# Bias rows loaded one unit ahead, and the weights of eleven attention units formed by VectorE into DRAM

## The chip, the cores and the metric

The kernel runs on one core of a Trainium2 chip. Its engines are TensorE (PE; its weight loads are shown as PEld), VectorE (DVE), ScalarE (ACT), GpSimd (POOL) and the DMA engines; nearly all DMAs are issued by SyncE (SP), whose queue is worked off in order, so a DMA that waits for something holds back all that stand behind it. The metric is the device time of one execution in microseconds (us). The kernel before takes 2162.34 us (median of three runs, 2156.7 to 2164.05).

## The reference

A decoder trunk of two layers on one sequence of 1024 positions with 1024 features, all float32. Layer 0 mixes positions by a gated MLP, layer 1 by dilated attention; each is followed by an MLP with squared ReLU (width 4096), with RMSNorm ahead of each part and at the end. The change concerns the attention:

```python
WINDOW_DILATIONS = ((128, 1), (512, 4), (2048, 16))
ATT_HEADS, HEAD_DIM = 8, 64
qkv = (h @ w_qkv).reshape(B, S, 3, N_DIL_GROUPS, ATT_HEADS, HEAD_DIM)
...
# for each of the three groups (window, dilation), with blk = window // dilation:
s = jnp.einsum('bnqrhc,bnkrhc->bnrhqk', qb, kc) * (HEAD_DIM ** -0.5)
rel = blk + jnp.arange(blk)[:, None] - jnp.arange(2 * blk)[None, :]
bias = jnp.transpose(bias_table[_t5_bucket(jnp.clip(rel, 0, blk) * dilation)], (2, 0, 1))
logits = jnp.where(valid, s + bias, NEG_INF)
m = jnp.max(logits, axis=-1)
p = jnp.exp(logits - m[..., None])
den = jnp.sum(p, axis=-1)
num = jnp.einsum('bnrhqk,bnkrhc->bnqrhc', p, vc)
# the groups' outputs are merged per head with weights exp(m - m_all), then
o = (num_sum / den_sum[..., None]).reshape(B, S, ATT_WIDTH)
return o @ w_out
```

The bias of a logit depends only on the distance of query and key, so for each head and group it is one row of numbers, and a tile of biases is that row shifted by one for each partition.

## The kernel before

*Arithmetic.* A float32 matmul is made of three fp32r matmuls: each operand is split into a rounded part `hi` and a rest `lo`, and hi*hi, hi*lo and lo*hi are added up in one PSUM bank. `split` (L211, L212) does this: ACT rounds (`hi`), and DVE, or the engine that is handed in, subtracts (`lo`). Large products use a scheme with seven half-size products of sums of blocks instead of eight; so "formed" weights are the four quarter blocks of a matrix, added and subtracted (four operations) into seven operands, each split into hi and lo.

*Attention.* It is worked in 12 units, four pairs of heads by three groups, the groups in the order 1, 2, 0 (`ORDER`). Unit i in the function `unit_qk(i)` makes its queries and keys by seven products with the weights w[1], 6, 5, 2, 7, 3, 4; `total` adds banks, `halves` splits the results into `q` and `k`. While these products run for unit i, generators work on the unit before: `scorer` (L1260 adds the bias and takes the maximum on DVE, L1262 takes the exponential on ACT), `turner` (transposes P and splits it), `valuer` (P times V, out of the bank by L1300 on ACT and L1301 on DVE into `N`), `exchange` (softmax statistics through DRAM: `sc`, back as `ex`, L1377) and `merge`. Before the units, `all_values` makes V for all units and writes it to DRAM (`vd`), from which `v_load` brings the part of one unit (L1155 to L1161).

*Weights of the units.* Units listed in `PREPARED` are formed early by `prepare`, with DVE's adds, split and written to DRAM (`wd`, L481); in the attention `unit_weights` only loads them (L1081). The first list is formed in the last part of the first mixer, the second in `all_values`. Units 0, 3, 6 and 9 are in neither: for these `unit_weights` loads the four raw blocks and forms them with GpSimd just before use (L1091 to L1100, and the `lo` of `split`). A unit's weight is brought by `more()`, seven ahead of use, into one of eight buffers.

*Bias.* `bias_tile` loads, at the start of each unit, the bias row of two heads from DRAM (`bvec`), each partition shifted by one (L1027; for group 2, half of it after a memset, L1030 and L1032), into a buffer `t`. A DVE copy (L1037) reverses it into a buffer `b`, of which there are two.

*What sets the order.* PE's order is written out by a planner (`flow`), which estimates a time for each matmul and lets the generators go on when their due time, in ns in `LAT` and `PACE`, has come. The order on DVE, ACT, POOL and SP comes from a scheduler that goes by the program's order and by priorities (`tc.high_priority`) of the operations that PE waits for. Each engine then works strictly in its order. Temporary half tiles come from a ring of 13 buffers `t` (`temp`, `rtemp`), larger ones from 37 buffers `s` (`slot`), raw weights from four buffers `r` (`raw`): whoever wants a buffer waits for the last use of what was in it, a DMA's landing included.

*The end of the attention.* When the weights have all been brought, `more()` steps through `end_loads`, which brings the outputs of earlier heads (`o<-od`, L1465), the last unit's V, the residual `h` (L1478) and the weights of the output projection (`wlbo`, L518).

## Time and profile before

| | |
|---|---|
| three runs | 2162.34, 2164.05, 2156.7 us |
| the profiled execution | 2172.37 us, its span 2170.6 us |
| busy: PE / DVE / ACT / POOL | 2124.0 / 1612.5 / 1115.9 / 571.3 us |
| granted TensorE clock, mean | 0.99 |
| moved by DMA | 345.65 MB |
| formed weights: written, loaded | 56 and 56 DMAs of 512 KB |
| the bias copies (L1037) | 12, from 1053.5 to 1426.3 us, 294 to 1552 ns each |

All times from a trace are of the profiled execution, which took longer than each of the three runs; differences are worked out within it and then set against the median. The attention's units run from about 1050 to 1510 us of the span. Busy time of PE near its whole share means that nothing can be gained in that stretch but by fewer matmuls; where it is less, or where the granted clock is under 1.00, the rows around that moment tell what PE waited for. "A <- B" in a row of waits reads: A was idle until B came.

### The profile page before, as it was taken

What the parts mean: (1) busy time and instruction counts of PE and PEld (TensorE: products, weight loads), DVE (VectorE), ACT (ScalarE), POOL (GpSimd) and SP (SyncE); (2) the same over time, 40 slices, a digit from 0 to 9 for tenths busy, and PEclk for the clock granted to TensorE, in tenths of its full rate; (3) what the DMA queues carried; (4) which work ended last, traced back from release to release, by engine and by line L of the source; (5) the groups of instructions that cost most, each with busy time, mean ns of one, the idle gap of its engine ahead of it and who ended that gap; (6) DMA issues with size and microseconds to landing.
All of it is one profiled execution on the core that took longest, in us unless ns stands there. A gap on an engine that the chain in (4) does not pass through costs nothing.

```text
span 2170.6 us, 30481 instructions
## 1 busy us (share of the span) xinstructions
PE 2124.0 (98%) x10192; PEld 1750.7 (81%) x10192; DVE 1612.5 (74%) x2965; ACT 1115.9 (51%) x2258; POOL 571.3 (26%) x414
## 2 busy tenths in 40 slices
PE   8999999999999999999999999999999999999997
PEld 7888887888878888788887777777788888788886
DVE  7867668777788776887457676758886667987776
ACT  7644436555564443345366555644455556544442
POOL 2000224333323233510220202001443332432244
PEclk9999999999999999999999999999999999999999
DMA  6324704566555443449734444491254443554432
GB/s 214 127 78 175 262 22 163 194 208 210 197 192 181 148 148 118 157 171 364 276 108 155 108 136 101 150 267 40 88 180 160 155 146 131 190 169 143 147 113 78
DMA packets 197825, 345.65 MB, mean 159 GB/s; under 512 B 36905, under 2 KB 64676, under 8 KB 197668
## 3 DMA queue, kind: packets, MB, share of 16 engines
q1 hardware_dynamic: 188528, 342.34, 47.3%
q10 hardware_dynamic: 9140, 1.36, 0.4%
q8 instruction: 80, 1.31, 0.2%
q14 instruction: 77, 0.63, 0.1%
HBM read 228.12 MB, written 115.51 MB: 158 GB/s over the span
## 4 chain that ended last, share of the span: by engine, by line
PE 79%; DVE 10%; DMA 5%; ACT 4%; issue 2%; POOL 0%; SPq 0%; ACTq 0%; DVEq 0%; POOLq 0%
PE at L183 43%; PE mm L183 35%; DMA t<-bvec 2%; ACT t L1262 1%; DVE tr L212 1%; PE at L190 1%; DVE h L311 1%; DVE N L1301 1%; DVE y L212 1%; DMA sc<-st 1%; DVE h L920 1%; DMA r<-in_w_v 1%; DVE wp L212 1%; DMA r<-in_w_dn 1%; DVE q L1189 1%
## 5 line engine op out<-in xcount | busy, mean ns | idle before, releaser
L211 ACT ACTIVATE wp<-r 128x512 fp32r<-128x512 f32 (+2 forms) x432 | 257.2, 598 | 356.0 <-PE at L183 236.2
L183 PE MATMUL at<-hx,wp 128*128 128x512 f32 x1740 | 406.3, 389 | 2.3 <-DVE h L920 2.0
L183 PEld LDWEIGHTS at<-hx,wp 128*128 128x128 f32 x1740 | 326.4, 188 | 71.6 <-DVE h L920 2.9
L212 DVE TENSOR_TENSOR wp<-r,wp 128x512 fp32r<-128x512 f32 (+2 forms) x404 | 308.3, 768 | 70.4 <-ACT wp L211 66.9
L183 PE MATMUL mm<-y,wp 128*128 128x512 f32 x1344 | 340.8, 396 | 2.0 <-issue 1.2
L183 PE MATMUL at<-t,wp 128*128 128x512 f32 x1344 | 313.7, 389 | 0.0
L183 PEld LDWEIGHTS mm<-y,wp 128*128 128x128 f32 x1344 | 249.8, 189 | 55.6 <-issue 2.2
L183 PEld LDWEIGHTS at<-t,wp 128*128 128x128 f32 x1344 | 252.3, 188 | 52.3
L354 POOL TENSOR_TENSOR t<-r 128x512 f32<-128x512 f32 (+3 forms) x62 | 87.7, 1414 | 580.6 <-DMA r<-in_w_dn 262.6
L267 POOL TENSOR_TENSOR t<-t 128x512 f32<-128x512 f32 (+1 forms) x64 | 84.3, 1317 | 440.2 <-ACT t L262 437.9
L183 PE MATMUL mm<-hx,wp 128*128 128x512 f32 x696 | 169.6, 390 | 0.4 <-DVE b L939 0.4
L183 PE MATMUL mm<-t,wp 128*128 128x512 f32 x576 | 158.7, 413 | 0.0
L183 PE MATMUL mm<-y,whi 128*128 128x512 f32 x512 | 158.2, 390 | 0.0
L212 DVE TENSOR_TENSOR hx<-t,hx 128x512 fp32r<-128x512 f32 x192 | 146.8, 771 | 11.6 <-ACT hx L211 11.3
L183 PEld LDWEIGHTS mm<-hx,wp 128*128 128x128 f32 x696 | 130.2, 188 | 29.3 <-issue 1.1
L211 ACT ACTIVATE hx<-t 128x512 fp32r<-128x512 f32 x192 | 118.8, 627 | 46.2 <-DMA t<-hid 40.0
L920 DVE TENSOR_TENSOR h<-h,at 128x512 f32<-128x512 f32 x144 | 98.0, 681 | 55.2 <-PE at L183 54.7
L183 PEld LDWEIGHTS mm<-t,wp 128*128 128x128 f32 x576 | 105.6, 194 | 22.2 <-issue 0.2
L183 PE MATMUL at<-y,wp 128*128 128x512 f32 x480 | 118.7, 390 | 0.0
L183 PEld LDWEIGHTS mm<-y,whi 128*128 128x128 f32 x512 | 95.6, 188 | 19.6
L1262 ACT ACTIVATE t<-t,st 128x128 f32<-128x128 f32 (+1 forms) x192 | 84.3, 440 | 44.7 <-DVE st L1260 44.0
L356 POOL TENSOR_TENSOR r<-r 128x512 f32<-128x512 f32 (+3 forms) x62 | 91.9, 1482 | 54.8 <-DVE wp L212 46.6
(210 smaller groups left out, 3561.5 us busy)
## 6 DMA issues: line engine op xcount, KB each, us to landing
t<-hid SPq DMA_DIRECT2D x182, 256.0 KB, 4.4
hid<-t SPq DMA_DIRECT2D x140, 256.0 KB, 2.3
r<-in_w_up SPq DMA_DIRECT2D x120, 256.0 KB, 2.7
wd<-wq SPq DMA_DIRECT2D x56, 512.0 KB, 3.9
wp<-wd SPq DMA_DIRECT2D x56, 512.0 KB, 3.3
r<-in_w_dn SPq DMA_DIRECT2D x80, 256.0 KB, 2.6
hid<-b SPq DMA_DIRECT2D x56, 256.0 KB, 2.7
r<-in_w_v SPq DMA_DIRECT2D x48, 256.0 KB, 2.9
```

Source lines behind the costliest of these rows:

```text
L183: nc.tensor.matmul(out, lhsT, rhs, **kw)
L190: nc.tensor.transpose(out, src, ident)
L211: nc.scalar.activation(hi, src, AF.Copy)
L212: (engine or nc.vector).tensor_tensor(lo, src, hi.bitcast(F32), op=ALU.subtract)
L267: nc.gpsimd.tensor_tensor(self.acc, self.acc, sq, op=ALU.add)
L311: nc.vector.tensor_tensor(x, x, ps, op=ALU.add)
L354: tt(r3, r[0, 0], r[1, 0], op=ALU.subtract)
L356: tt(r[1, 1], r[1, 0], r[0, 0], op=ALU.subtract)
L920: return engine.tensor_tensor(hs[i, s], hs[i, s], src, op=ALU.add).ins
L1189: nc.vector.scalar_tensor_tensor(lo, src, sc, hi.bitcast(F32), op0=ALU.mult, op1=ALU.subtract)
L1262: nc.scalar.activation(p[:, c], p[:, c], AF.Exp, bias=m, scale=-1.0, accum_out=dn)
L1301: nc.vector.tensor_tensor(o, o, pv[r, c], op=ALU.add)
```

## The change

1. `PREPARED` now lists eleven units in three lists: 1 to 5, then 6, 7, 8 and 10, then 9 and 11. So only unit 0 is formed with GpSimd. The first list starts earlier (ahead of column block 4 of the U product instead of 5 to 7), the third is new: it starts 20 us of the planner's time after the attention begins, at a pace of 3.5 us per step, with raw weights in the four `r` buffers.
2. In `prepare` a formed operand is split into two half tiles of the ring `t` and written as two DMAs of 256 KB, instead of one tile of the ring `s` and one DMA of 512 KB.
3. `bias_tile` only loads; the new `bias_turn` makes the reversed copy. Unit i+1's rows are loaded at the start of unit i, and copied in the middle of unit i, after the last scores of unit i-1.
4. `ex` is loaded 12 instead of 8 us (planned) after the statistics were written.
5. `end_loads` starts with the last unit's V instead of the outputs.

```diff
-PREPARED = ((1, 2, 4, 5), (7, 8, 10, 11))
-PACE = (2100.0, 2500.0, 1900.0)
-LAT = dict(..., ex=8000.0)
+PREPARED = ((1, 2, 3, 4, 5), (6, 7, 8, 10), (9, 11))
+PACE = (2100.0, 2500.0, 1900.0, 3500.0)
+LAT = dict(..., ex=12000.0)
...
-    def prepare(unit_list, pace):
+    def prepare(unit_list, pace, own=temp):
...
-            r00, r10, r01, r11 = (load(w_qkv[n + a][:, half(b)], temp()) for a, b in ((0, 0), (1, 0), (0, 1), (1, 1)))
+            r00, r10, r01, r11 = (load(w_qkv[n + a][:, half(b)], own()) for a, b in ((0, 0), (1, 0), (0, 1), (1, 1)))
             yield pace
             def put(p, src):
-                t = slot((P, 2, HALF), F32R, "wq")
-                split(t[:, 0, :], t[:, 1, :], src)
-                nc.sync.dma_start(wd[i, p], t.bitcast(F32))
+                hi, lo = rtemp(), rtemp()
+                split(hi, lo, src)
+                for e, t in enumerate((hi, lo)):
+                    nc.sync.dma_start(wd[i, p][:, e, :], t.bitcast(F32))
...
-        if tiles[-1] == 7:
+        if tiles[0] == 4:
             flow.add(prepare(PREPARED[0], PACE[0]))
...
+        return rev, w
+
+    def bias_turn(rev, w):
         t = spare().rearrange("p (a b) -> p a b", a=2)
         src = rev[:, 0:2 * w]
         nc.vector.tensor_copy(t[:, :, 0:w], bass.AP(tensor=src.tensor, offset=src.offset + w - 1,
...
-        u.bias = bias_tile(u.hp, g)
+        if i == 0:
+            u.bias = bias_turn(*bias_tile(u.hp, g))
         if i < NU - 1:
             flow.add(v_load(i))
+            U[i + 1].rev = bias_tile(U[i + 1].hp, U[i + 1].g)
...
             flow.until(lambda: U[i - 1].scored.t is not None)
+        if i < NU - 1:
+            U[i + 1].bias = bias_turn(*U[i + 1].rev)
         halves(1, 1, own(total(k1, e, k1), g))
...
     def end_loads():
+        flow.add(v_load(NU - 1))
+        flow.pump()
         for hp in range(2):
             outs_load(hp, 0)
-        flow.add(v_load(NU - 1))
         yield
...
         flow.add(gen())
+    flow.add(prepare(PREPARED[2], PACE[3], raw), 20000.0)
     for i in range(NU):
         unit_qk(i)
```

PE's order is the same in both kernels. The other engines' order moves in three places that matter.

SP's queue around the loads of bias rows for unit 6 before (`V` of units 4 and 5, raw weights `r` of unit 6, statistics `ex`, formed weights `wp` of unit 7, and `t<-bvec` for units 5 and 6):

```order
504 L1377 DMA ex_11646<-sc_11509 128x8x4
505 L1027 DMA t<-bvec 128x2x256
506 L1161 DMA V<-vd_8790 64x4x256 x4
507 L172 DMA r<-in_w_qkv 128x512 x3
508 L1155 DMA V<-vd_8790 128x4x256
509 L172 DMA r<-in_w_qkv 128x512
510 L1377 DMA ex_12009<-sc_11879 128x8x4
511 L1155 DMA V<-vd_8790 128x4x256
512 L1081 DMA wp<-wd_1_140 128x1024
513 L1027 DMA t<-bvec 128x2x256
514 L1081 DMA wp<-wd_6_143 128x1024
```

and now (the first `t<-bvec` holds unit 6's rows, the second unit 7's; `wp` are formed weights of units 6 and 7):

```order
543 L1165 DMA V<-vd_8921 64x4x256
544 L1028 DMA t<-bvec 128x2x256
545 L1085 DMA wp<-wd_1_147 128x1024
546 L1165 DMA V<-vd_8921 64x4x256
547 L1085 DMA wp<-wd_6_150 128x1024
548 L1165 DMA V<-vd_8921 64x4x256 x2
549 L1385 DMA ex_11948<-sc_11789 128x8x4
...
557 L1385 DMA ex_12300<-sc_12141 128x8x4
558 L1085 DMA wp<-wd_1_154 128x1024
559 L1033 DMA t<-bvec 64x2x64 x2
```

The rows of unit 6 are now issued where those of unit 5 were, ahead of `ex`; the raw weights of unit 6 are gone, and loads of formed weights stand among those of `V`.

DVE's order at the copy of unit 6's bias (L1189 is the `lo` of q and k, L1301 the addition into N, L1260 the score reduction, written as ISA):

```order
1352 L1194 TENSOR_TENSOR t<-t,mm 128x512
1353 L1189 SCALAR_TENSOR_TENSOR k_11818<-t,k_11817 128x512
1354 L1037 COPY b<-t 128x512
1355 L1301 TENSOR_TENSOR N<-N,at 64x256 x2
1356 L1260 ISA t,st_11930<-at,b 128x128
1357 L1260 ISA st_11930 128x1
```

and now:

```order
1391 L1309 TENSOR_TENSOR N<-N,at 64x256
1392 L1195 SCALAR_TENSOR_TENSOR k_12081<-t,k_12080 128x512
1393 L1041 COPY b<-t 128x512
1394 L1200 TENSOR_TENSOR t<-t,mm 128x512
1395 L1195 SCALAR_TENSOR_TENSOR q_12007<-t,q_12006 128x512
1396 L1309 TENSOR_TENSOR N<-N,at 64x256 x2
1397 L212 TENSOR_TENSOR tr<-at,tr 128x256 x2
1398 L1200 TENSOR_TENSOR t<-t,mm 128x512
```

The copy has moved up a few rows, and the rows that it copies were asked for a unit earlier.

DVE's order while the scores of unit 0 are reduced and unit 1's products run, before:

```order
1069 L1194 TENSOR_TENSOR t<-t,mm 128x512
1070 L1260 ISA t,st_10068<-at,b 128x128
1071 L1260 ISA st_10068 128x1
...
1076 L1260 ISA t,st_10068<-at,b 128x256
1077 L1260 ISA st_10068 128x1
1078 L1194 TENSOR_TENSOR t<-t,mm 128x512
1079 L212 TENSOR_TENSOR tr<-at,tr 128x384 x2
```

and now (`tr<-r,tr` is the `lo` of a formed weight of unit 9, `r<-r` an addition of its blocks):

```order
1092 L1200 TENSOR_TENSOR t<-t,mm 128x512
1093 L212 TENSOR_TENSOR tr<-r,tr 128x512
1094 L1268 ISA t,st_10265<-at,b 128x128
1095 L1268 ISA st_10265 128x1
...
1100 L1268 ISA t,st_10265<-at,b 128x256
1101 L1268 ISA st_10265 128x1
1102 L486 TENSOR_TENSOR r<-r 128x512
1103 L212 TENSOR_TENSOR tr<-r,tr 128x512
1104 L1200 TENSOR_TENSOR t<-t,mm 128x512
1105 L212 TENSOR_TENSOR tr<-at,tr 128x384 x2
```

Three operations of the new third list stand between the score reductions and the totals; 22 such operations are spread over the first units of the attention.

More of the change, by code (lines that the diff above doesn't have):

```diff
@@ L109 @@
 CALM = (1600.0, 1600.0, 1200.0, 1600.0)
-PREPARED = ((1, 2, 4, 5), (7, 8, 10, 11))
-PACE = (2100.0, 2500.0, 1900.0)
-LAT = dict(sum=2600.0, rms=2600.0, tile=1600.0, gate=8500.0, soft=5500.0, turn=4200.0, fe=1300.0, v=2000.0, qk=4200.0, merge=2600.0, out=700.0, fex=3.0, ve=1600.0, vd=6000.0, ex=8000.0)
+PREPARED = ((1, 2, 3, 4, 5), (6, 7, 8, 10), (9, 11))
+PACE = (2100.0, 2500.0, 1900.0, 3500.0)
+LAT = dict(sum=2600.0, rms=2600.0, tile=1600.0, gate=8500.0, soft=5500.0, turn=4200.0, fe=1300.0, v=2000.0, qk=4200.0, merge=2600.0, out=700.0, fex=3.0, ve=1600.0, vd=6000.0, ex=12000.0)
 @with_exitstack
@@ L465, in start_terms @@
         flow.add((terms.second if s else terms.first)(sq, gi), LAT["sum"])
-    wd = {(i, p): dram.tile([P, 2, HALF], F32, name=f"wd{i}_{p}", bufs=1) for i in PREPARED[0] + PREPARED[1] for p in SEVEN}
-    def prepare(unit_list, pace):
+    wd = {(i, p): dram.tile([P, 2, HALF], F32, name=f"wd{i}_{p}", bufs=1) for i in sum(PREPARED, ()) for p in SEVEN}
+    def prepare(unit_list, pace, own=temp):
         tt = nc.vector.tensor_tensor
```

## The prediction, made before the result was known

> **What bounds the kernel now.** I read the page's busy line and its chain first, then the busy time by stretches of the attention, then the waits, and last the rows in time around each stall of PE.

> ```profile
> PE 2124.0 (98%) x10192; PEld 1750.7 (81%) x10192; DVE 1612.5 (74%) x2965; ACT 1115.9 (51%) x2258; POOL 571.3 (26%) x414
> PE 79%; DVE 10%; DMA 5%; ACT 4%; issue 2%; POOL 0%; SPq 0%; ACTq 0%; DVEq 0%; POOLq 0%
> PE at L183 43%; PE mm L183 35%; DMA t<-bvec 2%; ACT t L1262 1%; DVE tr L212 1%; PE at L190 1%; DVE h L311 1%; DVE N L1301 1%; DVE y L212 1%; DMA sc<-st 1%; DVE h L920 1%; DMA r<-in_w_v 1%; DVE wp L212 1%; DMA r<-in_w_dn 1%; DVE q L1189 1%
> ```

> TensorE is busy for 98% of the span, and POOL, from which the change takes work, has no share in the chain. So only two things can move the time: matmuls, which the change does not touch, and the few places where PE stands or runs slowly. The chain names one of these: 2% for the landing of the bias rows (t<-bvec). The next rows are the attention in stretches of about 54 us: length, then busy time of PE, PEld, DVE, ACT and POOL, the granted clock, the DMA share and GB/s.

> ```profile
> 1086.00:1140.00 54.00, 53.83 (x337) 44.26 (x337) 32.80 (x107) 34.60 (x105) 13.04 (x10) 1.00 0.36 107
> 1140.00:1194.00 54.00, 52.58 (x336) 43.10 (x336) 40.61 (x133) 33.13 (x95) 1.28 (x1) 1.00 0.46 156
> 1194.00:1248.00 54.00, 50.77 (x300) 41.77 (x299) 33.33 (x86) 30.30 (x84) 15.51 (x11) 0.94 0.45 106
> 1248.00:1302.00 54.00, 48.82 (x297) 39.95 (x296) 37.95 (x129) 31.84 (x92) 0.00 (x0) 0.94 0.40 134
> 1302.00:1357.00 55.00, 51.78 (x304) 42.60 (x303) 33.95 (x87) 30.31 (x84) 14.21 (x10) 0.94 0.42 104
> ```

> In the first two stretches PE is nearly full at clock 1.00 and does 336 matmuls. In the next three it does about 300 and the clock is 0.94: there is the loss. The waits of 1085 to 1530 us (total, times, longest) name the cause:

> ```profile
> DVE b L1037 <- DMA t<-bvec: 31.3, 11, 8.3
> PE at L183 <- DVE N L1301: 11.9, 6, 4.6
> PE at L183 <- DMA V<-vd: 2.4, 1, 2.4
> ```

> DVE waits for bias rows, and behind its copy stands the addition N that empties the bank PE wants next. In time, first PE (start, length, and in brackets the idle time before and what ended it), then DVE:

> ```profile
> 1216.56 2.10 PE L183 MATMUL at<-k,q 64*128 64x128 f32 x12 [2.39 <-DVE N L1301]
> 1254.61 2.23 PE L183 MATMUL at<-k,q 64*128 64x256 f32 x12 [4.56 <-DVE N L1301]
> 1325.46 2.10 PE L183 MATMUL at<-k,q 64*128 64x128 f32 x12 [2.38 <-DVE N L1301]
> 1360.14 0.35 PE L183 MATMUL at<-k,q 64*128 64x256 f32 x1 [0.99 <-DVE N L1301]
> 1427.31 0.29 PE L183 MATMUL at<-k,q 64*128 64x128 f32 x1 [1.28 <-DVE N L1301]
> 1441.29 1.84 PE L183 MATMUL at<-tr,V 128*128 128x128 f32 x8 [2.41 <-DMA V<-vd]
> ```

> ```profile
> 1214.01 1.21 DVE L1037 COPY b<-t 128x512 f32<-128x512 f32 x1 [2.23 <-DMA t<-bvec]
> 1252.85 0.43 DVE L1037 COPY b<-t 128x512 f32<-128x512 f32 x1 [8.30 <-DMA t<-bvec]
> 1322.73 1.39 DVE L1037 COPY b<-t 128x512 f32<-128x512 f32 x1 [2.05 <-DMA t<-bvec]
> 1358.38 0.43 DVE L1037 COPY b<-t 128x512 f32<-128x512 f32 x1 [4.74 <-DMA t<-bvec]
> 1426.29 0.43 DVE L1037 COPY b<-t 128x512 f32<-128x512 f32 x1 [3.22 <-DMA t<-bvec]
> ```

> Each of the first five PE gaps ends a microsecond or two after such a late copy. Four of the six gaps are followed by a spell in which the clock is halved; the one in the last row of these is V's, and the fifth row here, after the 0.99 us gap, shows full clock.

> ```profile
> 1216.00:1223.00 7.00, 6.33 (x27) 5.47 (x28) 3.72 (x20) 5.05 (x20) 2.56 (x2) 0.51 0.11 24
> 1253.00:1261.00 8.00, 6.36 (x25) 5.05 (x26) 6.14 (x28) 4.86 (x19) 0.00 (x0) 0.57 0.18 68
> 1325.00:1332.20 7.20, 6.63 (x27) 5.77 (x28) 3.62 (x20) 5.11 (x21) 2.56 (x2) 0.53 0.07 15
> 1441.40:1451.60 10.20, 10.20 (x38) 8.32 (x39) 3.72 (x14) 3.69 (x13) 0.00 (x0) 0.50 1.03 394
> 1360.20:1367.00 6.80, 6.57 (x43) 5.50 (x44) 5.57 (x30) 5.09 (x20) 0.00 (x0) 1.00 0.31 110
> ```

> What a spell costs is its length times what is missing from the clock: 7.00 x 0.49 = 3.4, 8.00 x 0.43 = 3.4, 7.20 x 0.47 = 3.4, and 10.20 x 0.50 = 5.1 us. Gaps of 2.38 us and more bring one, gaps of 1.28 us and less do not.

> **The change, part by part.** *Bias rows a unit ahead.* The DMA keeps its place in the program, but what it loads is now the next unit's rows, and the copy stands in the middle of the unit before its use. Why the rows came late is seen on SP's queue before the worst stall:

> ```profile
> 1243.26 0.38 SPq L1377 DMA_DIRECT2D ex<-sc  x1
> 1243.73 1.74 SPq L1155 DMA_DIRECT2D V<-vd  x1
> 1245.56 0.46 SPq L1081 DMA_DIRECT2D wp<-wd  x1
> 1246.11 0.38 SPq L1027 DMA_DIRECT2D t<-bvec  x1
> ```

> Issued at 1246.11, they were copied at 1252.85, 6.7 us later. A unit lasts about 35 us (copies at 1322.73 and 1358.38), and the copy in the middle of the unit leaves more than 10 us between issue and copy, so even the 8.30 us wait is covered. Without its wait and its own length, the copy lets N run 3.4, 8.7, 3.4, 5.2 and 3.7 us earlier, each more than the PE gap behind it. So all five gaps go: 2.39 + 4.56 + 2.38 + 0.99 + 1.28 = 11.6 us, and their three spells, 10.3 us: -21.9 us. Bounds: -11.6 (the gaps go and the spells stay) and -21.9.

> [...]

> *Units 3, 6 and 9 no longer formed on GpSimd; eleven units formed by DVE.* This takes 33 POOL operations away and adds 33 to DVE; ACT's 7 roundings per unit only move in time.

> ```profile
> L212 POOL TENSOR_TENSOR wp<-r,wp 128x512 fp32r<-128x512 f32 x21 | 28.4, 1351 | 229.0 <-ACT wp L211 229.0
> L212 DVE TENSOR_TENSOR wp<-r,wp 128x512 fp32r<-128x512 f32 (+2 forms) x404 | 308.3, 768 | 70.4 <-ACT wp L211 66.9
> ```

> POOL's 28.4 us in the attention cost PE nothing that the chain shows, so their removal brings 0. Beside POOL's work the bias copy took 1.21 and 1.39 us instead of 0.43, but that is inside the gaps counted already.

> DVE's new operations take 33 x 0.768 = 25 us. Eleven of them go to the first list, which begins earlier in the first layer's mixer and has five units instead of four: 8.4 us. There DVE has room, as in the stretch

> ```profile
> 262.00:278.00 16.00, 16.00 (x72) 13.24 (x71) 1.74 (x4) 1.90 (x3) 3.87 (x3) 1.00 0.21 76
> ```

> with 1.74 us of DVE work in 16 and PE full: cost 0 (if the cover failed, 8.4). The other 22 go to the new third list (units 9 and 11), interleaved with the first units of the attention: 16.9 us. With the 73.4 us that DVE works in 1086 to 1194 this makes 90.3 of 108, and ACT gets 14 roundings more. It has room on average, but the order on DVE is fixed, so that each new operation stands ahead of a score reduction, a total or an N. It also shares the ring of 13 "t" buffers with them, and a buffer is now free only when the write of a weight half to DRAM has landed. The row nearest to such crowding is where DVE was fullest:

> ```profile
> 1165.00:1175.00 10.00, 10.00 (x65) 8.82 (x64) 9.62 (x30) 5.91 (x16) 0.00 (x0) 1.00 0.30 105
> 1175.00:1185.00 10.00, 9.09 (x61) 7.08 (x60) 6.49 (x25) 7.39 (x23) 0.00 (x0) 1.00 0.45 137
> ```

> DVE at 9.62 of 10 cost PE nothing in that stretch and 0.91 us in the next. The third list has two units of eight steps at a pace of 3.5 us, 56 us at the least; I take 80, four such pairs: 3.6 us; and one gap in two chances long enough for a spell, half of 3.4 us: 1.7. I take +5 us. Bounds: 0 (all in DVE's free time) and 16.9 (all on PE's path), before spells.

> *Writes in 256 KB halves instead of 512 KB, and three units more loaded from DRAM.* 56 writes become 154, loads of formed weights go from 56 to 77.

> ```profile
> wd<-wq SPq DMA_DIRECT2D x56, 512.0 KB, 3.9
> SPq L1081 <- PE mm L183: 122.5, 35, 11.1
> ```

> DMA engines are below half busy in all five attention rows above, a write is waited for by a buffer only, and SP mostly waits for PE, since eight weight buffers run ahead: cost 0, bounds 0 to 98 more issues x 0.38 us (a single issue above) = 37 us, if SP's queue were the last to arrive everywhere; the chain gives SP's own queue 0%. [...]

> *The later load of softmax statistics (8 to 12 us) and the order at the end.* ex<-sc no longer holds SP ahead of V and weights: 0, since the bias gap it fed is already counted. The V stall at 1441.29 stays: its V stands behind the same four h loads and two weight loads as before. The bias and ex issues ahead of these go,

> ```profile
> 1418.08 0.78 SPq L1027 DMA_DIRECT2D t<-bvec  x1
> 1423.88 0.58 SPq L1377 DMA_DIRECT2D ex<-sc  x1
> ```

> which is 1.4 us, but PE arrives 1.28 us earlier without the gap at 1427.31. So 0; the bounds are -7.5 (2.41 + 5.1) and 0.

> **Sum.** -21.9 + 5 = -16.9 us. The profiled execution took 2172.4 us and would take 2155.5; it lies 10.0 us above the median of the runs, 2162.3, from which the same difference gives 2145.4: forecast 2145 us. [...] The likeliest case's own range is 2140 (crowding 0) to 2152 (crowding 12).

> **The rivals.** *The spells stay (A).* If the half clock has another cause than the gaps, for instance the short matmuls of 64 rows that follow each of them, only the gaps go: -11.6 + 3.6 = -8, 2154 us. For it speaks that the gaps are shorter than the spells; against it that none of the short matmuls after 0.99 us was slowed.

> *The V stall goes too (B).* Then 2145 - 7.5 = 2138 us. For it: 1.4 us less stands ahead on SP; against it: PE comes 1.3 us earlier, and the DMA engines are full there (1.03).

> *V comes late elsewhere (C).* Units 3, 6 and 9 now have weight loads on SP that wait for PE, up to 11.1 us each, with V behind them. One V stall like that of 1441.29 costs 7.5 us: 2153 us. For it: these units had no such loads before. Against it: the one V that PE waited for came through full DMA engines (1.03), and they are below half busy in all five attention rows.

> *Crowding on DVE (D), the other side.* The 22 operations and the landings of 28 half writes come ahead of score reductions in units 0 to 3. If one of these steps is late by more than PE's banks cover, PE gets a gap like the 2.39 us one with its spell, 5.8 us. Four of them (23 us) eat the whole gain; this is the point from which it decides. Four or about that: 2156 to 2169, no change. Six: 35 - 21.9 = +13, 2175 us. For it: DVE was at 9.62 of 10 in 1165 to 1175 already, and each new rounding is a pair of ACT and DVE with a wait between. Against it: PE stood full there, and DVE is free for 34.6 of the 108 us.

> **How the numbers follow.** Measurement tells 0.3%, 6.5 us, from no change. Forecast case 0.40, A 0.11, B 0.13, C 0.10, D without a change 0.10, D slower 0.16. Faster: 0.40 + 0.13 + 0.10 and 0.07 of A, which ends near the bound, 0.70; same: 0.10 and the rest of A, 0.14; slower 0.16. The range runs from 2135, a little under B, to 2168, the upper part of D; it leaves out D's six stalls (about 0.13) and little below.

> **What would show it.** Right: the copy's wait for t<-bvec near 0 instead of 31.3 us, no gap before N of over 1 us in the attention after 1200, clock 1.00 in the stretches now at 0.94, some 336 matmuls in each, and PE's loss at V still there. Wrong: PE gaps behind score reductions, totals or weight splits between about 1095 and 1200, with a clock under 1.00 in the two stretches that are now full; or a new wait for V; or half clock without a gap. The crowding term is the weakest: nothing in the trace has this work in this place.

## The result and the profile after

The changed kernel takes 2149.31 us (median of five runs, 2147.96 to 2151.17), the kernel before 2162.72 us (2156.7 to 2166.88): ratio 0.9938, 95% interval 0.992 to 0.9957. It is 13.4 us faster, by the interval 9.3 to 17.3; forecast were 17. The profiled execution took 2148.0 us, against 2172.4 before.

The busy line, the chain by engines and the chain by lines, after:

```profile
PE 2111.2 (98%) x10192; PEld 1740.0 (81%) x10192; DVE 1629.2 (76%) x2998; ACT 1116.2 (52%) x2258; POOL 521.4 (24%) x381
PE 80%; DVE 10%; ACT 4%; DMA 4%; issue 2%; SPq 0%; POOL 0%; ACTq 0%; DVEq 0%; POOLq 0%
PE at L183 43%; PE mm L183 36%; PE at L190 1%; DVE tr L212 1%; DVE h L311 1%; DMA r<-in_w_v 1%; DMA V<-vd 1%; DVE h L921 1%; DVE y L212 1%; DVE wp L212 1%; ACT t L1270 1%; DVE N L1309 1%; DMA wd<-tr 1%; DVE t L1437 0%; ACT q L1194 0%
```

The landing of bias rows, 2% of the span before, is gone from the chain; the same matmuls keep PE busy for 13 us less, since fewer of them run at half clock (mean granted clock 0.996, before 0.990). DMA wd<-tr, the writes of formed weights, has come in at 1%. The attention in stretches, with the columns of the prediction's table:

```profile
1078.00:1132.00 54.00, 51.21 (x294) 40.55 (x294) 34.99 (x95) 31.17 (x84) 0.00 (x0) 0.97 0.90 274
1132.00:1186.00 54.00, 51.42 (x322) 41.64 (x320) 42.70 (x135) 35.02 (x98) 0.00 (x0) 1.00 0.70 218
1186.00:1240.00 54.00, 53.20 (x339) 44.01 (x340) 38.64 (x117) 32.85 (x103) 0.00 (x0) 1.00 0.66 179
1240.00:1294.00 54.00, 53.58 (x344) 44.07 (x342) 40.54 (x135) 34.37 (x98) 0.00 (x0) 1.00 0.47 146
1294.00:1348.00 54.00, 53.29 (x334) 43.75 (x334) 36.32 (x107) 29.80 (x89) 0.00 (x0) 1.00 0.72 192
```

The picture is turned round. From 1186 to 1348 us PE does 334 to 344 matmuls in 54 us at full clock, where it did about 300 at 0.94. The first two stretches, which were nearly full, have lost: 51.2 and 51.4 us busy, and a clock of 0.97 in the first. (These stretches do not start at the same matmul as those of the prediction's table; the next section compares the same matmuls.) The waits of 1040 to 1510 us:

```profile
DVE b L1041 <- DMA t<-bvec: 10.0, 1, 10.0
DVE r L485 <- DMA r<-in_w_qkv: 8.8, 2, 5.9
DVE tr L212 <- DMA wd<-tr: 1.9, 1, 1.9
PE at L190 <- ACT t L1270: 2.4, 1, 2.4
```

One copy out of twelve still waits for its rows, that of unit 0, whose rows are loaded where they are copied; PE has no gap from 1050 to 1082 us, so it lost nothing by it here. All other copies start with no wait. The new loss in the first stretch is one row of PE, and behind it one of DVE; the second stretch loses by small gaps, none over 0.92 us.

```profile
1125.71 1.49 PE L190 MATMUL at<-ident,t 128*128 128x128 f32 x4 [2.38 <-ACT t L1270]
```

```profile
1124.23 0.69 DVE L485 TENSOR_TENSOR r<-r 128x512 f32<-128x512 f32 x1 [5.93 <-DMA r<-in_w_qkv]
```

The third list's first addition for unit 11 stands in DVE's order ahead of a score reduction; it waits 5.93 us for raw weights, the scores and their exponential wait behind it, and PE stands for 2.38 us. This is the old stall, with raw weights in place of bias rows. The gap before V, which had cost 2.41 us, is 0.58 us in this execution:

```profile
1423.09 1.08 PE L183 MATMUL at<-tr,V 128*128 128x128 f32 x8 [0.58 <-DMA V<-vd]
```

### The profile page after: what moved, and what is told of

It is laid out like the page before. It is cut to its first block, busy times and chain, and to the rows that moved or that the text cites. A ratio compares the mean times of both kernels' runs of the same rounds, so it can differ in the third digit from the quotient of the medians.

```text
span 2146.3 us, 30685 instructions
## 1 busy us (share of the span) xinstructions
PE 2111.2 (98%) x10192; PEld 1740.0 (81%) x10192; DVE 1629.2 (76%) x2998; ACT 1116.2 (52%) x2258; POOL 521.4 (24%) x381
## 3 DMA queue, kind: packets, MB, share of 16 engines
q1 hardware_dynamic: 205664, 364.37, 51.2%
## 4 chain that ended last, share of the span: by engine, by line
PE 80%; DVE 10%; ACT 4%; DMA 4%; issue 2%; SPq 0%; POOL 0%; ACTq 0%; DVEq 0%; POOLq 0%
PE at L183 43%; PE mm L183 36%; PE at L190 1%; DVE tr L212 1%; DVE h L311 1%; DMA r<-in_w_v 1%; DMA V<-vd 1%; DVE h L921 1%; DVE y L212 1%; DVE wp L212 1%; ACT t L1270 1%; DVE N L1309 1%; DMA wd<-tr 1%; DVE t L1437 0%; ACT q L1194 0%
## 5 line engine op out<-in xcount | busy, mean ns | idle before, releaser
L211 ACT ACTIVATE wp<-r 128x512 fp32r<-128x512 f32 (+2 forms) x411 | 244.0, 597 | 346.1 <-PE at L183 222.0
L183 PE MATMUL at<-hx,wp 128*128 128x512 f32 x1740 | 406.3, 389 | 2.2 <-DVE h L921 2.0
L183 PEld LDWEIGHTS at<-hx,wp 128*128 128x128 f32 x1740 | 326.3, 188 | 71.6 <-DVE h L921 2.8
L212 DVE TENSOR_TENSOR wp<-r,wp 128x512 fp32r<-128x512 f32 (+2 forms) x404 | 308.9, 770 | 67.9 <-ACT wp L211 64.5
L183 PE MATMUL mm<-y,wp 128*128 128x512 f32 x1344 | 338.9, 395 | 1.9 <-issue 1.1
L183 PE MATMUL at<-t,wp 128*128 128x512 f32 x1344 | 313.7, 389 | 0.0
L183 PEld LDWEIGHTS at<-t,wp 128*128 128x128 f32 x1344 | 252.3, 188 | 52.4
L183 PEld LDWEIGHTS mm<-y,wp 128*128 128x128 f32 x1344 | 248.4, 188 | 54.5 <-issue 2.2
L183 PE MATMUL mm<-hx,wp 128*128 128x512 f32 x696 | 169.6, 390 | 0.7 <-DVE hx L212 0.3
L183 PE MATMUL mm<-y,whi 128*128 128x512 f32 x512 | 158.3, 390 | 0.0
L212 DVE TENSOR_TENSOR hx<-t,hx 128x512 fp32r<-128x512 f32 x192 | 148.7, 782 | 11.6 <-ACT hx L211 11.5
L183 PEld LDWEIGHTS mm<-hx,wp 128*128 128x128 f32 x696 | 130.2, 188 | 29.6 <-issue 1.0
L183 PE MATMUL mm<-t,wp 128*128 128x512 f32 x576 | 154.1, 403 | 0.0
L211 ACT ACTIVATE hx<-t 128x512 fp32r<-128x512 f32 x192 | 118.7, 627 | 44.2 <-DMA t<-hid 39.3
L183 PEld LDWEIGHTS mm<-t,wp 128*128 128x128 f32 x576 | 102.6, 188 | 21.4
L183 PE MATMUL at<-y,wp 128*128 128x512 f32 x480 | 118.7, 390 | 0.0
L183 PEld LDWEIGHTS mm<-y,whi 128*128 128x128 f32 x512 | 95.6, 188 | 19.5
L183 PEld LDWEIGHTS at<-y,wp 128*128 128x128 f32 x480 | 89.9, 188 | 19.9 <-issue 1.3
## 6 DMA issues: line engine op xcount, KB each, us to landing
wp<-wd SPq DMA_DIRECT2D x77, 512.0 KB, 4.6
```

The lines of the kernel that those rows point to most:

```text
L183: nc.tensor.matmul(out, lhsT, rhs, **kw)
L211: nc.scalar.activation(hi, src, AF.Copy)
L212: (engine or nc.vector).tensor_tensor(lo, src, hi.bitcast(F32), op=ALU.subtract)
```

## The experiments

Medians of runs, and ratios to the kernel before with 95% intervals. The first four kernels shared a chip, so did the next four and the last four.

| kernel | median us (lowest to highest) | ratio |
|---|---|---|
| bias rows alone | 2144.15 (2141.24 to 2154.06) | 0.9902 (0.9882 to 0.9922) |
| weights alone | 2168.41 (2164.67 to 2171.36) | 1.0012 (1.0 to 1.0024) |
| change, end order put back | 2150.81 (2148.18 to 2153.43) | 0.9928 (0.9911 to 0.9945) |
| change, longer wait after raw loads | 2151.05 (2147.99 to 2154.46) | 0.9927 (0.991 to 0.9943) |
| bias rows, ex and end order | 2143.36 (2142.86 to 2143.59) | 0.9882 (0.986 to 0.9904) |
| change without third list | 2148.12 (2146.04 to 2155.86) | 0.9911 (0.9888 to 0.9933) |
| change, raw weights early | 2147.11 (2144.23 to 2148.17) | 0.9897 (0.9877 to 0.9917) |
| made stalls | 2289.73, one run | |
| the change again | 2148.71 (2146.38 to 2150.53) | 0.9913 (0.9892 to 0.9934) |
| bias rows, ex and end order again | 2143.61 (2142.56 to 2144.2) | 0.9889 (0.9869 to 0.991) |
| change, whole tiles | 2155.54 (2153.5 to 2158.75) | 0.9945 (0.9921 to 0.9968) |
| no third list, unit 0's rows early | 2143.52 (2142.02 to 2152.96) | 0.9895 (0.9871 to 0.992) |

The kernel before was itself spread over 2157.71 to 2173.3, 2163.07 to 2177.16 and 2160.83 to 2179.87 us in these three series, which is what makes the ratios' intervals 0.4% wide. Kernels of one series are better set against each other by their own runs; across series a difference of a few us says little.

The traces allow a sharper comparison. PE's 10192 matmuls come in the same order in all these kernels but the one with made stalls, so the time from one matmul to another can be compared. The table has the time in us between the starts of matmuls 4946 and 5507 (1100 to 1190 us before, where the third list works), 5507 and 5749 (to 1235, the middle of it GpSimd's work for unit 6), and 6171 and 6351 (1310 to 1345, GpSimd's work for unit 9):

| kernel (one trace each) | third list's stretch | unit 6's | unit 9's |
|---|---|---|---|
| before | 89.98 | 45.04 | 34.96 |
| the change again | 97.26 | 39.20 | 28.90 |
| bias rows, ex and end order again | 88.13 | 40.67 | 30.32 |
| change without third list | 88.10 | 39.20 | 30.29 |
| change, raw weights early | 94.06 | 39.20 | 28.87 |

Traces of kernels with the same parts agree within 0.2 us here: the change's first trace has 97.18, 39.20 and 28.87, bias rows alone 88.11, 40.68 and 30.35. The times of the kernel before hold its bias gaps and their spells as well.

**Bias rows alone.** The kernel before with the new `bias_tile` and `bias_turn` and nothing else:

```diff
-        u.bias = bias_tile(u.hp, g)
+        if i == 0:
+            u.bias = bias_turn(*bias_tile(u.hp, g))
         if i < NU - 1:
             flow.add(v_load(i))
+            U[i + 1].rev = bias_tile(U[i + 1].hp, U[i + 1].g)
...
+        if i < NU - 1:
+            U[i + 1].bias = bias_turn(*U[i + 1].rev)
         halves(1, 1, own(total(k1, e, k1), g))
```

> Only the bias rows are loaded a unit ahead; units 3, 6 and 9 are still formed with GpSimd, ex and the end loads stand as before. Theory 1 (the five waits of the copy for its rows are the gain): the five PE gaps before N and their three spells go, the chain loses t<-bvec, the V gap of 2.4 us near 1440 stays; 13 to 20 us less than before. Theory 2 (the gain is GpSimd's work and its raw weight loads, which held SP's queue up): under 4 us less than before. Spells of half clock without a gap of over 2 us ahead would speak for neither.

The ratio gives 2162.7 x 0.0098 = 21 us (17 to 25 by its interval), a little over what theory 1 expected and far above theory 2. One thing that theory 1 named failed: the V gap near 1440 us, which was to stay, is not in this trace, so that the 21 us may hold a share of it. By the same matmuls the part from 1190 to 1370 us of before, with the first four gaps and their three spells, went from 180.16 to 161.84 us, 18.3 us less. What is left of the wait for additions into N, in 1085 to 1530 us, where it had been 11.9 us in 6 waits:

```profile
PE at L183 <- DVE N L1308: 0.9, 2, 0.4
```

GpSimd works in this kernel as before. So the gain before the V gap is that of the bias rows. The median is under that of the whole change, but the intervals overlap; the two are set against each other on one chip further on.

**Weights alone.** The three lists and the half writes, with bias rows, `ex` and the end as before.

```diff
-PREPARED = ((1, 2, 4, 5), (7, 8, 10, 11))
+PREPARED = ((1, 2, 3, 4, 5), (6, 7, 8, 10), (9, 11))
...
-                t = slot((P, 2, HALF), F32R, "wq")
-                split(t[:, 0, :], t[:, 1, :], src)
-                nc.sync.dma_start(wd[i, p], t.bitcast(F32))
+                hi, lo = rtemp(), rtemp()
+                split(hi, lo, src)
+                for e, t in enumerate((hi, lo)):
+                    nc.sync.dma_start(wd[i, p][:, e, :], t.bitcast(F32))
```

> The three lists and the half writes alone; bias rows, ex and the end loads as before. Theory 1: the copies still wait for their rows and PE still has gaps before N; added to these is the new gap near 1123 us, where DVE waits 5.9 us for raw weights of the third list: 3 to 6 us slower than before. Theory 2: 9 to 13 us faster, POOL idle in the attention and the clock near 1.00.

0 to 0.24% slower, up to 5 us: close to theory 1 and far from theory 2. Taking away GpSimd's additions and its raw loads brought at most what the crowding took. The gap near 1123 us that theory 1 named is not there; the copies go on waiting for their rows, now at other units, and the worst stall has moved to 1152:

```profile
1151.11 0.43 DVE L1038 COPY b<-t 128x512 f32<-128x512 f32 x1 [5.75 <-DMA t<-bvec]
```

```profile
1152.87 2.23 PE L183 MATMUL at<-k,q 64*128 64x256 f32 x12 [4.89 <-DVE N L1302]
```

**End order put back.**

```diff
-        flow.add(v_load(NU - 1))
-        flow.pump()
         for hp in range(2):
             outs_load(hp, 0)
+        flow.add(v_load(NU - 1))
         yield
```

> The changed kernel with only the order of the end loads put back (outputs first, then the last unit's V). Theory 1 for the V gap (it went because the last unit's V and then the h loads are issued earlier): the gap of 2.4 us and its spell of 5.1 us come back, 4 to 8 us slower than the changed kernel. Theory 2 (it went because bias rows and ex no longer stand ahead): no gap, within 2 us of the changed kernel.

The gap before V came back, but not the spell, and the median is 1.5 us above the change's, which was measured in another series, and within both kernels' spread:

```profile
1424.39 0.86 PE L183 MATMUL at<-tr,V 128*128 128x128 f32 x6 [2.87 <-DMA V<-vd]
```

Neither theory is met whole. Over all runs this gap does not go by the end order: bias rows alone keeps the old order and has no such gap; the last experiment has the new order and a gap of 2.17 us. All have full DMA engines there (a share of 1.00 to 1.13 in the 3 to 4 us around PE's arrival), and PE's waits for V seen in before, the change, the old end order and the last experiment are 2.41, 0.58, 2.87 and 2.17 us. What decides it in one execution stays open.

**Longer wait after raw loads.**

```diff
-            yield pace
+            yield pace if own is temp else 4 * pace
```

> The changed kernel, with 14 instead of 3.5 us of the planner's time between the raw loads of the third list and its first addition. Theory 1 (the gap of 2.4 us near 1123 comes from the raw weights of unit 11 landing late ahead of a score reduction on DVE): gap and spell go, 3 to 5 us faster than the changed kernel. Theory 2 (DVE is crowded by the 22 operations, whichever stands first): a gap of like size turns up at another place in units 1 to 4, within 1.5 us of the changed kernel or slower.

As theory 2 said in its numbers, but by theory 1's mechanism: the planner's longer wait moved the addition and the loads of raw weights together (the last load is issued at 1132.48 us, in the change by 1117.43), and the addition waits again, at another score:

```profile
1137.10 0.69 DVE L485 TENSOR_TENSOR r<-r 128x512 f32<-128x512 f32 x1 [3.75 <-DMA r<-in_w_qkv]
```

```profile
1138.59 0.44 PE L190 MATMUL at<-ident,t 128*128 128x128 f32 x2 [2.42 <-DVE st L1268]
```

This gap of 2.42 us brought no spell (granted clock 1.00 from 1130 to 1144 us); the last section takes that up. So the experiment told the two theories not apart.

**Bias rows, ex and end order.** Bias rows alone, with `ex=12000.0` and the new `end_loads`:

```diff
-LAT = dict(..., ex=8000.0)
+LAT = dict(..., ex=12000.0)
```

> The bias rows a unit ahead, the later ex and the new order of the end loads, with the weights as before (units 0, 3, 6, 9 on GpSimd, whole-tile writes). Theory 1 (the weights part of the change costs what the changed kernel lacks against bias rows alone): like bias rows alone, 0.989 to 0.992 of before. Theory 2 (ex and the end order cost it): 0.993 to 0.995, like the changed kernel.

Theory 1, a little beyond its range. Ex and the end order cost nothing that can be seen: the same matmuls, from 1060 to 1460 us of before, take 371.27 us here and 371.13 with bias rows alone.

**The change without its third list.**

```diff
-PREPARED = ((1, 2, 3, 4, 5), (6, 7, 8, 10), (9, 11))
+PREPARED = ((1, 2, 3, 4, 5), (6, 7, 8, 10, 11), ())
```

> The changed kernel without the third list: unit 11 is formed in the second list, which has five units, and unit 9 with GpSimd as before. Theory 1 (the third list's operations and raw loads among the first units cost 5 us or more): 3 to 7 us faster than the changed kernel, 0.990 to 0.992 of before, no gap near 1123 us. Theory 2 (the cost is the half writes in the ring t, or the loads of formed weights on SP, and holds all through): within 2 us of the changed kernel.

The time speaks for theory 2, the trace for theory 1 with a new loss beside it. No gap is left near 1123 us, and the third list's stretch takes 88.10 us, as with the old weights. But there is a new gap at unit 0, behind the one copy whose rows are not loaded ahead; with its spell it makes the 40 us before that stretch 4.3 us longer. Why this copy's wait costs PE here and not in the change, where it was longer, stays open.

```profile
1078.85 0.43 DVE L1041 COPY b<-t 128x512 f32<-128x512 f32 x1 [6.06 <-DMA t<-bvec]
```

```profile
1081.57 2.75 PE L183 MATMUL mm<-t,wp 128*128 128x512 f32 x8 [2.34 <-DVE t L1200]
```

**Raw weights early.** Unit 11's raw blocks are loaded with unit 9's, into two buffers of the ring `s` (`raws` is the load of the four blocks):

```diff
-            r00, r10, r01, r11 = (load(w_qkv[n + a][:, half(b)], own()) for a, b in ((0, 0), (1, 0), (0, 1), (1, 1)))
+            if own is temp:
+                r00, r10, r01, r11 = raws(i, own)
+            elif i == unit_list[0]:
+                r00, r10, r01, r11 = raws(i, own)
+                two = [slot((P, 2, HALF), F32, "rw") for _ in range(2)]
+                nxt = iter([two[0][:, 0, :], two[0][:, 1, :], two[1][:, 0, :], two[1][:, 1, :]])
+                early = raws(unit_list[1], lambda: next(nxt))
+            else:
+                r00, r10, r01, r11 = early
```

> The changed kernel, with the raw weights of unit 11 in two slots of the ring s, loaded together with those of unit 9 before the first unit is scored, so that no DVE addition can wait for them. The operations stay where they are. Theory 1a (the cost of the third list is this one late transfer): the gap of 2.4 us and its spell go, 3 to 6 us faster than the changed kernel. Theory 1b (it is also the crowding: 22 operations and writes that hold the ring t): some gaps of 1 to 3 us stay in 1100 to 1190, gain under 3 us.

The gap near 1123 us is gone, and the median is some 2 us under the change's (2149.31 and, further on, 2148.71, in other series; the runs overlap); in the trace the third list's stretch is 3.2 us shorter. Small gaps behind the crowded DVE stay:

```profile
1112.40 0.39 PE L183 MATMUL at<-tr,V 128*128 128x256 f32 x1 [0.71 <-ACT tr L211]
1113.68 0.56 PE L183 MATMUL at<-tr,V 128*128 128x256 f32 x3 [0.90 <-DVE tr L212]
```

These two together brought a spell of 3.4 us at 1114.22. That is theory 1b, though the gaps are under the 1 to 3 us that it named: the late transfer is a part of the cost, some 2 us by the medians and 3.2 in the trace, and the rest, 5.9 us against the old weights, is crowding.

**Made stalls.** Bias rows alone, with ten made waits of PE in each MLP:

```diff
+    def stall(n):
+        ps, t = at_bank(), temp()
+        matmul(ps[:, 0:P], ones, ident, start=True, stop=True)
+        with tc.high_priority(offset=PRIO):
+            for _ in range(n):
+                nc.scalar.activation(t[:, 0:P], ps[:, 0:P] if _ == 0 else t[:, 0:P], AF.Copy)
+        matmul(ps[:, P:P + 1], t[:, 0:P], ones[:, 0:1], start=True, stop=True)
...
             product(a, w[1], x.t[1])
+            if 4 <= q < 14:
+                stall(q - 3 if layer else 14 - q)
```

> Bias rows ahead alone, and in each MLP ten made waits of PE: after the first product of ten stages a small matmul, a chain of 1 to 10 copies on ACT that starts with its result, and a matmul that needs the end of the chain (growing in the second MLP, shrinking in the first). The results are not used. If a gap of some 2.4 us always brings a spell of half clock, as the four in the kernel before seemed to say, all gaps above that have one of 3.4 us or more and none below 1.3 us has. [...] Some 60 to 110 us slower, of which the gaps are 20 x 0.5 to 5 us.

It was 145 us slower than bias rows alone (one run, on another chip), more than expected: the gaps in the first MLP were up to 7.6 us long, and each took a spell with it. Of the twenty, the shortest had no spell; the next and all longer ones had one:

```profile
1676.51 0.38 PE L183 MATMUL at<-ones,t 128*128 128x1 f32 x2 [2.00 <-ACT t L754]
```

```profile
1723.49 0.38 PE L183 MATMUL at<-ones,t 128*128 128x1 f32 x2 [2.51 <-ACT t L754]
```

In this dense stage the expectation is not refuted; gaps in the attention that do refute it, and what decides, are in the last section, from all the traces.

**The change again, and bias rows, ex and end order again**, on one chip.

> The changed kernel itself, on the chip of the next ones, so that they can be set against it directly. Around 2149 us; the gap near 1123 us is there again, with or without its spell.

> Bias rows ahead, later ex and end order, weights as before, a second time. Theory 1 (forming and loading the weights of three more units by DVE costs some 5 us): 2142 to 2145 us, 4 to 8 us under the changed kernel on the same chip. Theory 2 (the difference was that of the chips): within 2 us of it.

2148.71 and 2143.61 us, in ranges that do not meet (2146.38 to 2150.53, and 2142.56 to 2144.2). So the weights part of the change costs 5.1 us net, theory 1, and the kernel without it beats both kernels of the case: 0.9889 of before. In the change's second trace the gap near 1123 us is there again, 2.54 us at 1125.09, with a spell of 3.4 us. The stretches of 1078 to 1186 us in the kernel without the weights part, where the change had 51.2 and 51.4 us of PE:

```profile
1078.00:1132.00 54.00, 54.00 (x338) 44.24 (x336) 33.46 (x106) 35.55 (x103) 11.77 (x9) 1.00 0.44 130
1132.00:1186.00 54.00, 53.56 (x345) 44.04 (x344) 40.93 (x135) 34.40 (x98) 2.79 (x2) 1.00 0.47 150
```

The table above shows what these 5.1 us are made of. The third list's stretch is 9.1 us longer with the list; without the list, in the otherwise whole change, it is as short as with the old weights. But units 6 and 9 are 1.5 and 1.4 us shorter where GpSimd does not form their weights; the kernel without third list, which leaves unit 9 alone to GpSimd, has the short time at unit 6 and the long one at unit 9. The rows of the kernel without the weights part, around unit 6's, show how GpSimd reaches PE:

```profile
1206.92 2.08 POOL L1095 TENSOR_TENSOR r<-r 128x512 f32<-128x512 f32 x1
1209.04 0.63 ACT L211 ACTIVATE wp<-r 128x512 fp32r<-128x512 f32 x1 [2.72 <-POOL r L1095]
1209.69 0.38 ACT L1307 ACTIVATE N<-at 64x256 f32<-64x256 f32 x1
1210.10 0.42 DVE L1308 TENSOR_TENSOR N<-N,at 64x256 f32<-64x256 f32 x1 [1.93 <-ACT N L1307]
1210.67 0.29 PE L183 MATMUL at<-k,q 64*128 64x128 f32 x1 [0.41 <-DVE N L1308]
```

ACT's rounding of a weight waits 2.72 us for GpSimd's sum, the copy of N out of the bank stands behind it on ACT, DVE's addition behind that, and PE behind the addition. Just before, DVE's split of k took 1.91 us beside GpSimd's work, as it took 1.94 in the kernel before (at 1209.84 us); in the change it takes 1.15 (at 1216.59 us).

**Whole tiles.** The change, with `put` as before: one tile of the ring `s`, one DMA of 512 KB.

```diff
-                hi, lo = rtemp(), rtemp()
-                split(hi, lo, src)
-                for e, t in enumerate((hi, lo)):
-                    nc.sync.dma_start(wd[i, p][:, e, :], t.bitcast(F32))
+                t = slot((P, 2, HALF), F32R, "wq")
+                split(t[:, 0, :], t[:, 1, :], src)
+                nc.sync.dma_start(wd[i, p], t.bitcast(F32))
```

> The changed kernel, with the formed operands again in one tile of the ring s and written by one DMA of 512 KB. Theory 1 (the late raw weights and DVE's order are the cost): within 2 us of the changed kernel. Theory 2 (writes that hold the ring t are the cost): 3 to 6 us faster, and no waits of totals or score steps for wd.

Neither: it is 7 us slower than the change. In the attention the ring `s` is in use by V, q, k and N, and ACT waits for its buffers until a write has landed; DVE waits behind ACT (3.38 us for a `wq` at 1155.82 us), N behind DVE, PE behind N. From the waits of 1040 to 1200 us, and PE:

```profile
ACT wq L211 <- DMA wd<-wq: 8.8, 4, 3.0
```

```profile
1157.85 2.23 PE L183 MATMUL at<-k,q 64*128 64x256 f32 x12 [4.11 <-DVE N L1308]
```

So the half writes through the ring `t` belong to a third list in the attention; they are no cost beside this.

**No third list, unit 0's rows early.** The change without its third list, with this on top:

```diff
             if r == 1:
                 flow.add(prepare(PREPARED[1], PACE[2]))
+            if r == 2:
+                U[0].rev = bias_tile(U[0].hp, U[0].g)
...
         if i == 0:
-            u.bias = bias_turn(*bias_tile(u.hp, g))
+            u.bias = bias_turn(*u.rev)
```

> The changed kernel without the third list (unit 11 in the second, unit 9 on GpSimd), and with the bias rows of unit 0, the only ones that are still loaded where they are copied, loaded during the last third of the value stage. Theory 1 (a copy that waits for its rows on DVE is what stops PE, at unit 0 as elsewhere): the 2.3 us gap near 1079 us and its spell go, 3 to 5 us faster than without this step, 2143 to 2145 us. Theory 2 (DVE is simply full there): the gap stays, within 1.5 us.

Theory 1 by its time: 4.6 us faster than without the step (on another chip), and level with the best kernel, 2143.61, on the same chip. The trace bears out half of that: no copy makes PE wait any more, but a gap of 1.78 us for formed weights at 1079.78 stands in the old one's place, without a spell, so that the 40 us at unit 0 are 2.1 us longer than in the change instead of 4.3. There is one more gap, of 2.17 us, for V. This step was not tried together with the third list; in the change PE lost nothing at unit 0.

## Why the prediction was right, and where it was not

*Bias rows, -21.9 us.* Right in mechanism and in size. All five gaps went, and the stretches have the clock and the matmuls that were named. By the same matmuls, from 1060 to 1430 us of before, the kernel with the old weights and the new bias rows gains 22.2 us; 1.8 of them are small waits ahead of the five gaps, and up to 3 us that the term counted stay, as GpSimd's. Bias rows alone gave 21 us by the medians.

*Crowding, +5 us.* Right in place, before 1200 us, and too small, though inside its bounds: the third list's stretch is 9.1 us longer with the list than without (7.3 longer than in the kernel before, where bias rows already cost 1.8). The mechanism was half named: 22 operations ahead of score reductions were counted, but the single largest piece, 4.1 us with its spell (2.38 us of gap, and half of 3.41 us), was a DVE addition that waits for raw weights, which the prediction did not list; of the waits it did list, for writes to land, 1.9 us show up. It was the same fault that the change removed for the bias rows, put in again for raw weights.

*GpSimd's work, 0.* This step failed. The prediction took it that POOL's work cost PE nothing, since POOL has no share in the page's chain, and counted the slow bias copies beside it with the gaps. With the bias rows early, units 6 and 9 still lose 1.5 and 1.4 us where GpSimd forms their weights, and not where it does not: 2.9 us. Between GpSimd and PE stood ACT and DVE, so the page's shares did not show it.

*The first list, 0, half writes, 0, ex and end order, 0.* Right as far as the traces show. The matmul at 1060.04 us of before, behind the first list, starts at 1059.69 and 1059.30 us in the change's two traces, and at 1057.77 to 1059.51 in those with only bias rows, ex or end order changed, so that up to 2 us can be hidden there. Half writes beat whole ones in the third list.

*The V gap, 0.* Not settled, as measured above: in both traces of the change it went (rival B), but also where only the bias rows were changed, so it cannot be put down to the end order. With it the two profiled executions differ by 24.4 us.

*The sum.* By the traces the parts are -22.2 + 9.1 - 2.9 = -16.0 us up to 1430 us, where -16.9 were forecast. That they agree so well is luck in part: two terms were off, by 4 and by 3 us, in opposite directions. The medians differ by 13.4 us (9.3 to 17.3), and on the later chip by 15.7 (14 to 23); both intervals hold 16, so the medians single out no term. Nor was it shown that the -16.9 us, worked out in one execution, may be set against a median 10 us shorter: which gaps and spells that one has is not on record, and the median of the kernel before moved between 2162.7 and 2169.6 us from series to series.

*Rival A* (gaps go, spells stay) fell: from 1190 to 1370 us the gaps alone are 10.3 us, and 18.3 were gained with bias rows alone, 21.3 with the change. *Rival C* (V late elsewhere) did not show. *Rival D* was right as a cost and wrong as an outcome: one gap with a spell of the kind that it priced at 5.8 us turned up (4.1 us here), not four.

## What to carry to other kernels

In a queue that is worked in order, ask of each instruction whose data come by DMA what stands behind it: a copy of 0.4 us that nobody needed yet stopped TensorE for 4.6 us because an addition stood behind it, and the cure here was to issue the load a unit earlier (21 us by the medians). An engine without a share in the chain can still hold others up: work taken off GpSimd brought 2.9 us. Put onto DVE where DVE feeds TensorE, the same kind of work cost 9 us, and where TensorE had no need of DVE, nothing that shows. Try the parts of a change one by one, since a sum that comes out right can hold two errors, and the best kernel was a part of the change.

## What the runs showed of the hardware

```profile
1437.99:1441.41 3.42, 1.01 (x5) 0.53 (x5) 0.69 (x1) 0.44 (x1) 0.00 (x0) 1.00 1.10 223
1441.41:1444.82 3.41, 3.41 (x14) 3.01 (x15) 0.68 (x2) 0.38 (x1) 0.00 (x0) 0.50 1.04 350
```

```profile
1419.60:1423.01 3.41, 1.92 (x9) 1.24 (x7) 0.69 (x1) 1.46 (x7) 0.00 (x0) 1.00 1.00 175
1423.01:1426.43 3.42, 2.04 (x15) 1.88 (x15) 0.51 (x2) 0.45 (x2) 0.00 (x0) 1.00 1.06 213
1426.43:1429.84 3.41, 3.41 (x26) 2.78 (x24) 3.13 (x13) 2.30 (x9) 0.00 (x0) 1.00 1.03 391
```

The gap of 2.41 us fell into one window, which had 1.01 us of work, and the clock was halved. The longer gap of 2.87 us fell across two, which had 1.92 and 2.04 us, and nothing happened. The gap of 2.42 us with the longer wait fell across windows of 1.94 and 2.47 us of work and had no spell either, and two gaps of 0.71 and 0.90 us in one window had one (raw weights early, 1.81 us of work). So the prediction's reading, that gaps of 2.38 us and more bring a spell, held in the trace of before only by how its gaps lay on the grid. Counted over all traces between 20 us from the start and 15 us from the end: each of 30 windows at full clock with under 1.5 us of work was followed by half clock, 8 of 34 with 1.5 to 2.1 us were (in the traces of before and of the change's first run alone 5 of 5, and 1 of 7), and above that none but those of the next paragraph. What decides between 1.5 and 2.1 us stays open. The grid also gives one way in which the same program can lose a spell of 3.4 us in one execution and not in the next; the kernel before, with four gaps of over 2 us in the attention, was spread over 14 to 19 us in a series, the best kernel over less than 2 us. But bias rows alone, with no such gap there in its trace, was spread over 13 us, and that the grid is the cause of the spread was not tried.

Matmuls with one column did not keep the clock up here. In the output projection of the kernel before, the profile has PE busy throughout, and the clock fell all the same, after a window with 24 of them:

```profile
1506.26:1509.67 3.41, 3.41 (x29) 3.29 (x28) 1.14 (x2) 1.50 (x3) 0.69 (x1) 1.00 0.64 235
1509.67:1513.09 3.42, 3.42 (x9) 2.64 (x9) 1.33 (x6) 0.25 (x1) 0.00 (x0) 0.50 0.50 181
```

```profile
1506.83 2.79 PE L183 MATMUL at<-ones,t 128*128 128x1 f32 x24
```

The 24 matmuls, the sums of squares of a norm, take 2.79 us, and their spell costs another 1.7. The best kernel has that spell too, at 1480 us. In the change's first trace the grid cuts the same matmuls in two, 17 in one window and 7 in the next, and there is no spell. In all traces, 13 of 14 windows with 20 or more of them were followed by one.
